# Idle matmuls and a new order of loads in the first stage of a one-core transformer block

## The chip, the core and the metric

The kernel runs on one core of one Trainium2 chip. The metric is the device time of one execution in microseconds (us); less is better. A core has five engines with instruction queues of their own: TensorE (PE in the profile, with its weight loads as PEld), VectorE (DVE), ScalarE (ACT), GpSimd (POOL) and SyncE (SP), which here only issues loads and stores to the DMA engines.

## What is computed

One block on x [256, 2048], all in float32, with a conditioning vector c [2048]:

```python
mod = jax.nn.silu(c) @ w_ada + b_ada              # 2048 -> 6 * 2048
shift_m, scale_m, gate_m, shift_f, scale_f, gate_f = split(mod, 6)
h = rms_norm(x, pre_norm_mix) * (1 + scale_m) + shift_m
q_n, k_c, ..., q_m, k_m, v_m = split(h @ w_in)    # eleven projections
o = concat(nsa_mixer(...), moba_mixer(...)) @ w_o
x = x + gate_m * rms_norm(o, post_norm_mix)
h = rms_norm(x, pre_norm_ffn) * (1 + scale_f) + shift_f
f = square(relu(h @ w_up)) @ w_down
x = x + gate_f * rms_norm(f, post_norm_ffn)
```

What matters for this change is the first line and the two after it, up to the first projections, and the last line.

## The kernel before, in words

**Order of the work.** The kernel is a list of units. A unit has a load (its DMA, issued on SP's queue into one of 5 raw buffers of 1 MB), a prep (work on what was loaded) and a main (its products). `Stream.run` (L108) issues loads in list order as raw buffers come free, preps up to four units ahead, and mains in order. The framework then lays out the order on each engine when the kernel is built: by priority, which follows the order of issue and is raised inside `tc.high_priority()`, among what its own plan holds to be ready. So a late-issued small instruction can stand early (L253 belongs to a later stage and runs at 1.37 us), but on the chip each engine takes its instructions in the order laid out.

**The modulation sums.** `shift` and `scale` for a group of k-tiles of h (M_MODS, L47: groups of 2, 4, 4, 4 and 2 tiles of 128 columns) are the product of silu(c) with a strip of w_ada. silu(c) is `csil` [128, 16], one column for each of the 16 k-tiles of the 2048 rows. `gemv_units` (L289) loads the strip (units of 4 or 2 k-tiles, SP at L305) and VectorE adds it up, `acc += w * csil[:, k]` (L318 for the first k-tile, L323 for the others). For the first group alone the k-tiles of M_DIRECT (L51) go to TensorE instead: `column_sums` (L352) runs 2 * nk = 4 matmuls of one column each into one PSUM bank, with w as the stationary side (L359); in the trace these are 8 instructions, since a float32 matmul stands there as two and a transpose as one. At the end of the group (`reduce`, L368) the running sum goes through the same function against a column of ones, another 8. The bank is opened by a matmul of the bias with the identity (L356). L389 and L390 then give `red`, and `main` (L393) modulates the transposed x with it (L400, L414). Later groups are reduced by transposes (L377) and split into a high and a low float32r part (L417, L418).

**x.** `x_units` (L566), one for each half t of 128 rows: load (L573), squares with their sum on ScalarE into `junk` (L579), 1/rms by `rstd_of` (L265: reduce, multiply-add, power on GpSimd), scaling on VectorE (L584), then 16 transposes through PSUM (L283; the identity they need is made by POOL at the start, masks.py:199) and copies by ScalarE (L285). `junk` and the running sum `acc` share one buffer (pool gp, tag "ga", one slot), so each waits for the one before it.

**The first products.** The projections of the first two k-tiles are done in plain float32 (M_PLAIN, L497): in_kv, in_kw, in_qn, in_vm, in_km, in_qm, with 1 MB of w_in each (0.5 for kw). The loads of the second modulation group (mods[1], eight loads of 1 MB and a last unit that reduces) are put between them by `spread` (L1000): in_kv, M0, M1, in_kw, M2, M3, in_qn, M4, M5, in_vm, M6, M7, in_km, in_qm in order of loads. Later products are `products` (L548): three float32r matmuls of high and low parts, whose weights are split by ScalarE (L544) and VectorE (L545).

**The end.** The last products end with `down_done` (L1222: square and sum on ScalarE, gating product on VectorE) for each 512 columns n of each half t, and `finish` (L1232): the four partial sums are added (L269), L273, power (L274), four scalings (L1238) and the stores.

**Lines that the change touches:** M_DIRECT (L51), the constants and silu(c) (L202 to L214), `columns` (L216), `column_sums`, `direct` and `reduce` (L352 to L391), `x_units` (L575 to L589), the list of units (L970 to L1000), `down_done` and `finish`.

## Time and profile before

| | us |
|---|---|
| median of 3 runs (1189.11 to 1192.91) | 1190.44 |
| the profiled execution | 1188.98 |
| its span, first to last instruction | 1187.2 |
| PE busy, share of the span | 1154.3 (97%) |
| DVE busy, share of the span | 901.4 (76%) |
| ACT busy, share of the span | 592.8 (50%) |
| HBM read | 308.99 MB |

Times in the rows are us from the first instruction, mean durations ns where so marked. A row `12.62 0.59 PE L356 MATMUL modm0t<-cola,ident ... x2 [3.62 <-DVE cola L223]` reads: at 12.62, for 0.59 us, two instructions of line 356 on TensorE wrote modm0t from cola and ident, after 3.62 us idle that ended with VectorE's line 223. Engines with a q behind them are issues to a queue. PE's ends are modelled, so the distance between starts is the firmer number.

### The profile page before, as it was taken

To read this page: it belongs to the slowest core of one execution; us is meant where nothing else is said; L and a number is where in the kernel's file an instruction comes from. 1 tells how busy PE (TensorE), PEld (TensorE's weight loads), DVE (VectorE), ACT (ScalarE), POOL (GpSimd) and SP (SyncE) were. 2 spreads that over 40 slices of the span, in tenths; PEclk is the share of its full clock that TensorE was granted. 3 is DMA by queue.
4 is the path that set the end of the run, shared out by engine and by line. 5 is a ranking of instruction groups with operands and counts; after the bars stand their busy time and mean duration, and the time that the engine had idled before them with its cause. 6 is when DMAs were issued, how large, how long until landed. Compare 5 with 4: busy or idle time off the path is not lost.

```text
span 1187.2 us, 14413 instructions
## 1 busy us (share of the span) xinstructions
PE 1154.3 (97%) x5411; PEld 935.7 (79%) x5411; DVE 901.4 (76%) x1111; ACT 592.8 (50%) x908; POOL 13.5 (1%) x23
## 2 busy tenths in 40 slices
PE   5999999999999998999999999999999999999997
PEld 4468888877777786888888888888888888888885
DVE  5679999889999988777888986666576666665573
ACT  4353444438746658565343344767444434444441
POOL 1000000000000001000000000000000000000000
PEclk9999999999999999999999999999999999999999
DMA  9999998775867985988878976545677777775541
GB/s 333 370 394 326 334 362 295 238 281 176 316 213 258 327 337 200 367 285 305 290 249 300 315 248 204 172 152 208 238 244 270 255 258 264 259 268 187 203 142 71
DMA packets 92601, 312.03 MB, mean 263 GB/s; under 512 B 6306, under 2 KB 14962, under 8 KB 79602
## 3 DMA queue, kind: packets, MB, share of 16 engines
q1 hardware_dynamic: 92324, 311.04, 74.7%
q8 instruction: 42, 0.69, 0.2%
q14 instruction: 27, 0.22, 0.1%
q10 hardware_dynamic: 208, 0.07, 0.0%
HBM read 308.99 MB, written 2.10 MB: 262 GB/s over the span
## 4 chain that ended last, share of the span: by engine, by line
PE 88%; DVE 7%; ACT 1%; issue 1%; DMA 1%; POOL 0%; SPq 0%; DVEq 0%; POOLq 0%; ACTq 0%
PE dps L550 10%; PE dps L551 10%; PE dps L549 10%; PE up L551 9%; PE up L550 9%; PE up L549 9%; PE wo L550 2%; PE wo L549 1%; PE wo L551 1%; PE ft L1146 1%; PE in_qm L551 1%; PE in_qm L549 1%; PE in_qm L550 1%; PE in_km L549 1%; PE in_km L550 1%
## 5 line engine op out<-in xcount | busy, mean ns | idle before, releaser
L323 DVE SCALAR_TENSOR_TENSOR modm<-modm,csil,modm 128x1024 f32<-128x1024 f32 (+1 forms) x72 | 78.3, 1087 | 9.4 <-DMA modm<-in_w_ada_dram 8.0
L323 DVE SCALAR_TENSOR_TENSOR modf<-modf,csil,modf 128x1024 f32<-128x1024 f32 x60 | 76.8, 1280 | 5.6 <-DMA modf<-in_w_ada_dram 5.2
L1162 DVE TENSOR_TENSOR facc<-up,facc 128x512 f32<-128x512 f32 x96 | 61.5, 685 | 19.2 <-PE up L551 19.2
L323 DVE SCALAR_TENSOR_TENSOR gatef<-gatef,csil,gatef 128x1024 f32<-128x1024 f32 x32 | 40.6, 1280 | 1.7 <-DMA gatef<-in_w_ada_dram 1.7
L323 DVE SCALAR_TENSOR_TENSOR gatem<-gatem,csil,gatem 128x1024 f32<-128x1024 f32 x32 | 40.3, 1275 | 0.0
L1202 DVE TENSOR_TENSOR flo<-facc,fhi 128x512 fp32r<-128x512 f32 x32 | 21.8, 686 | 2.0 <-ACT fhi L1201 2.0
L1201 ACT CAST fhi<-facc 128x512 fp32r<-128x512 f32 x32 | 19.7, 624 | 5.3 <-PE up L550 1.9
L1164 ACT ACTIVATE facc<-facc 128x512 f32<-128x512 f32 x32 | 18.4, 623 | 2.8 <-DVE facc L1162 2.8
L1160 ACT COPY facc<-up 128x512 f32<-128x512 f32 x32 | 18.0, 586 | 1.7 <-PE up L551 1.0
L545 DVE TENSOR_TENSOR up_13lo<-up,up_13hi 128x1024 fp32r<-128x1024 f32 x8 | 9.8, 1226 | 11.5 <-ACT up_13hi L544 11.5
L545 DVE TENSOR_TENSOR up_14lo<-up,up_14hi 128x1024 fp32r<-128x1024 f32 x8 | 9.8, 1226 | 11.1 <-ACT up_14hi L544 11.1
L1151 ACT ACTIVATE facc<-ft 128x512 f32<-128x512 f32 x32 | 17.1, 586 | 0.4 <-PE ft L1146 0.2
L1146 PE MATMUL ft<-ident,facc 128*128 128x128 f32 x128 | 16.8, 273 | 0.0
L1146 PEld LDWEIGHTS ft<-ident,facc 128*128 128x128 f32 x128 | 14.7, 140 | 2.6 <-ACT facc L1151 0.4
L544 ACT CAST up_7hi<-up 128x1024 fp32r<-128x1024 f32 x8 | 8.4, 1056 | 14.2 <-PE up L551 14.2
L544 ACT CAST up_11hi<-up 128x1024 fp32r<-128x1024 f32 x8 | 8.4, 1056 | 14.2 <-PE up L551 14.2
L544 ACT CAST up_10hi<-up 128x1024 fp32r<-128x1024 f32 x8 | 8.4, 1056 | 13.3 <-PE up L551 13.3
L544 ACT CAST up_6hi<-up 128x1024 fp32r<-128x1024 f32 x8 | 8.4, 1056 | 13.3 <-PE up L551 13.3
L544 ACT CAST up_14hi<-up 128x1024 fp32r<-128x1024 f32 x8 | 8.4, 1049 | 12.6 <-PE up L551 12.6
L544 ACT CAST up_9hi<-up 128x1024 fp32r<-128x1024 f32 x8 | 8.4, 1056 | 12.1 <-DVE up_8lo L545 6.7
L544 ACT CAST up_8hi<-up 128x1024 fp32r<-128x1024 f32 x8 | 8.4, 1054 | 11.7 <-PE up L551 11.7
L544 ACT CAST up_5hi<-up 128x1024 fp32r<-128x1024 f32 x8 | 8.4, 1056 | 11.2 <-PE up L551 7.8
(2266 smaller groups left out, 3966.4 us busy)
## 6 DMA issues: line engine op xcount, KB each, us to landing
up<-in_w_up_dram SPq DMA_DIRECT2D x64, 1024.0 KB, 5.2
dn<-in_w_down_dram SPq DMA_DIRECT2D x64, 1024.0 KB, 5.0
modf<-in_w_ada_dram SPq DMA_DIRECT2D x64, 512.0 KB, 6.2
modm<-in_w_ada_dram SPq DMA_DIRECT2D x48, 512.0 KB, 7.1
gatem<-in_w_ada_dram SPq DMA_DIRECT2D x16, 1024.0 KB, 5.5
wo<-in_w_o_dram SPq DMA_DIRECT2D x16, 1024.0 KB, 6.3
gatef<-in_w_ada_dram SPq DMA_DIRECT2D x16, 1024.0 KB, 4.9
modm<-in_w_ada_dram SPq DMA_DIRECT2D x32, 256.0 KB, 6.0
```

What stands on the lines that cost most here:

```text
L323: nc.vector.scalar_tensor_tensor(part, w[:, j:j + step], csil[:, k:k + 1], part, ALU.mult, ALU.add)
L544: nc.scalar.copy(hi[:, 0:n], src)
L545: nc.vector.tensor_sub(lo[:, 0:n], src, hi[:, 0:n].bitcast(F32))
L549: nc.tensor.matmul(o, shi, whi, start=first, stop=False)
L550: nc.tensor.matmul(o, shi, wlo, start=False, stop=False)
L551: nc.tensor.matmul(o, slo, whi, start=False, stop=last)
L1146: nc.tensor.transpose(b[:, (2 * i + t) * P:(2 * i + t + 1) * P], f[:, t, (2 * j + i) * P:(2 * j + i + 1) * P], ident)
L1160: nc.scalar.copy(dst, b)
L1162: nc.vector.tensor_add(dst, b, dst)
L1164: nc.scalar.activation(dst, dst, AF.Relu)
L1201: nc.scalar.copy(hi, f)
L1202: nc.vector.tensor_sub(lo, f, hi.bitcast(F32))
```

## The change

Seven edits:

- silu(c) gets a buffer of its own, `sig`, in the pool and tag of the squares' `junk`, so the squares wait for it; the loads of b_ada and the two norm vectors move from the top into `load_columns`, issued behind the first load of w_ada, and `columns` becomes a unit between the second and third loads of the first group.
- `keep_warm` issues transposes of data at hand into a PSUM bank that nobody reads: 56 of the identity at the start, 24 of x behind the second half's transposes, and 4 of the weights behind each direct k-tile.
- M_DIRECT names six k-tiles (2, 5, 8, 11, 13, 14) in place of three, so ten are left to VectorE.
- The bias of the first group is added by VectorE behind the sums and no longer by a matmul ahead of them.
- The second half of x is scaled by ScalarE.
- The second group's loads are put at fixed places: in_kv, M0, in_kw, M1, in_qn, M2, M3, in_vm, M4, in_km, M5, M6, in_qm, M7 in order of loads, the reducing unit behind in_qm's first k-tile.
- At the end, the sum of squares of the first three column blocks is reduced and scaled once n = 2 is done, and the last block takes one multiply-add and the power.

```diff
--- before.py
+++ after.py
@@ -48,7 +48,9 @@
 
 M_PLAIN = 2
 
-M_DIRECT = (3, 7, 11)
+M_DIRECT = (2, 5, 8, 11, 13, 14)
+
+WARM = (56, 24, 4)
 F_MODS = (4, 4, 4, 4)
 F_GROUPS = ((0, 4), (4, 8), (8, 12), (12, 16))
 
@@ -203,15 +205,26 @@
     stageb = accp.tile([64, P], F32, tag="acc", name="stageb")
     stagec = accp.tile([16, P], F32, tag="acc", name="stagec")
     nc.scalar.dma_start(stagec, c.rearrange("b (r p) -> (b r) p", p=P))
-    nc.scalar.dma_start(stagea[0:96, :], b_ada.rearrange("b (r p) -> (b r) p", p=P))
-    nc.scalar.dma_start(stagea[96:112, :], g_pm.rearrange("b (r p) -> (b r) p", p=P))
-    nc.scalar.dma_start(stagea[112:128, :], g_pf.rearrange("b (r p) -> (b r) p", p=P))
     with tc.high_priority():
         pc = bank("pconst0")
         nc.tensor.transpose(pc[:, 0:16], stagec, ident[0:16, 0:16])
-        sigmoid_parts(csil, pc[:, 0:KD])
-        nc.vector.reciprocal(csil, csil)
-        nc.vector.tensor_mul(csil, csil, pc[:, 0:KD])
+
+        sig = gp.tile([P, KD], F32, tag="ga", name="csig")
+        sigmoid_parts(sig, pc[:, 0:KD])
+        nc.vector.reciprocal(sig, sig)
+        nc.vector.tensor_mul(csil, sig, pc[:, 0:KD])
+    warm = mbank("warm")
+
+    def keep_warm(src, n):
+        for i in range(n):
+            nc.tensor.transpose(warm[:, (i % 4) * P:(i % 4 + 1) * P], src, ident)
+
+    keep_warm(ident, WARM[0])
+
+    def load_columns():
+        nc.scalar.dma_start(stagea[0:96, :], b_ada.rearrange("b (r p) -> (b r) p", p=P))
+        nc.scalar.dma_start(stagea[96:112, :], g_pm.rearrange("b (r p) -> (b r) p", p=P))
+        nc.scalar.dma_start(stagea[112:128, :], g_pf.rearrange("b (r p) -> (b r) p", p=P))
 
     def columns():
 
@@ -351,16 +364,16 @@
 
         def column_sums(w, v, stop):
 
-            if "b" not in sums:
+            fresh = "b" not in sums
+            if fresh:
                 sums["b"] = bank(f"{name}t")
-                nc.tensor.matmul(sums["b"][:, 0:2 * nk].rearrange("p (s k) -> p s k", s=2), ident,
-                                 bias[:, :, ks], start=True, stop=False, skip_group_check=True)
             for i in range(2 * nk):
                 nc.tensor.matmul(sums["b"][:, i:i + 1], w[:, i * P:(i + 1) * P], v,
-                                 start=False, stop=stop, skip_group_check=True)
+                                 start=fresh and i == 0, stop=stop, skip_group_check=True)
 
         def direct(k, w):
             column_sums(w, csil[:, k:k + 1], False)
+            keep_warm(w[:, 0:P], WARM[2])
 
         units = gemv_units(name, base + k0 * P, W, True, min(1024 // W, 4), acc, first,
                            direct if tag == "m" and k0 == 0 else None)
@@ -385,9 +398,10 @@
                 return lambda k: (red[:, k - k0:k - k0 + 1], red[:, nk + k - k0:nk + k - k0 + 1])
             with tc.high_priority():
                 column_sums(acc.t, one, True)
-                b = sums["b"]
-                nc.vector.tensor_mul(red[:, nk:], b[:, nk:2 * nk], gcol[:, ks])
-                nc.vector.tensor_copy(red[:, 0:nk], b[:, 0:nk])
+                nc.vector.tensor_add(red.rearrange("p (s k) -> p s k", s=2),
+                                     sums["b"][:, 0:2 * nk].rearrange("p (s k) -> p s k", s=2),
+                                     bias[:, :, ks])
+                nc.vector.tensor_mul(red[:, nk:], red[:, nk:], gcol[:, ks])
             return lambda k: (red[:, k - k0:k - k0 + 1], red[:, nk + k - k0:nk + k - k0 + 1])
 
         def main():
@@ -581,12 +595,17 @@
             with tc.high_priority():
                 r = rstd_of(f"xr{t}", ss)
                 for v in st["x"]:
-                    nc.vector.tensor_scalar(v, v, r, None, ALU.mult)
+                    if t:
+                        nc.scalar.mul(v, v, r)
+                    else:
+                        nc.vector.tensor_scalar(v, v, r, None, ALU.mult)
 
         def main():
             if t == 0:
                 xnm.extend(pair(f"xnm{i}") for i in range(KD // 2))
             transposed(f"xt{t}", lambda k: st["x"][k // 8][:, (k % 8) * P:(k % 8 + 1) * P], xnm, t)
+            if t:
+                keep_warm(st["x"][1][:, 0:P], WARM[1])
 
         u = Unit(None, prep, main)
         u.begin = load
@@ -967,7 +986,6 @@
     k0s = np.cumsum((0,) + M_MODS).tolist()
     mods = [mod_units("m", k0, n, xnm, hstat) for k0, n in zip(k0s, M_MODS)]
     xu = [x_units(0), x_units(1)]
-    columns()
     gm = gate_units("m", g_qm, gate_m)
 
     def call(f):
@@ -991,13 +1009,16 @@
 
     def load_first():
         load0()
+        load_columns()
         for u in xu:
             u.begin()
 
     m0[0].load = load_first
-    stream.add(xu + m0)
+    stream.add(xu + m0[:2] + [Unit(None, columns)] + m0[2:])
     base = flat(in_units(n, 0, 2) for n in ("kv", "kw", "qn", "vm", "km")) + turn0[:2]
-    stream.add(spread(base, mods[1], 1, len(base) - 1))
+    for j, at in enumerate((2, 5, 8, 9, 12, 15, 16, 18, 19)):
+        base[at:at] = mods[1][j]
+    stream.add(base)
     base = turn0[2:] + flat(in_units(n, 2, 6) for n in ("km", "vm", "qn", "kw")) + turn1[:4]
     base.insert(3, Unit(None, late_constants))
     stream.add(spread(base, mods[2], 0, len(base) - 3))
@@ -1227,12 +1248,26 @@
             nc.vector.tensor_add(b, dps[0, 0], b)
         junk = pair("junk").rearrange("p a b -> p (a b)")
         nc.scalar.activation(junk, b, AF.Square, accum_out=fsq[t][:, n:n + 1])
+        if n >= 2:
+            with tc.high_priority():
+                final_rstd(n, t)
         nc.vector.tensor_mul(fg[n][:, t, :], b, gate_f["G"][:, n * 512:(n + 1) * 512])
+
+    frstd = [[sm.tile([P, 1], F32, name=f"fr{t}{i}", bufs=1) for i in range(2)] for t in range(NT)]
+
+    def final_rstd(n, t):
+
+        s, r = frstd[t]
+        if n == 2:
+            nc.vector.tensor_reduce(s, fsq[t][:, 0:3], axis=AX.X, op=ALU.add)
+            nc.vector.tensor_scalar(s, s, 1.0 / D, EPS, ALU.mult, ALU.add)
+        else:
+            nc.vector.tensor_scalar(r, fsq[t][:, 3:4], 1.0 / D, s, ALU.mult, ALU.add)
+            nc.gpsimd.tensor_tensor(r, r, mhalf, ALU.pow)
 
     def finish(t):
         x2 = x2h["x"]
-        with tc.high_priority():
-            r = rstd_of(f"fr{t}", fsq[t])
+        r = frstd[t][1]
         for n in range(4):
             cs = slice(n * 512, (n + 1) * 512)
             nc.vector.scalar_tensor_tensor(x2[:, t, cs], fg[n][:, t, :], r, x2[:, t, cs],
```

## Rows read from the trace of the kernel before

**Rows 1.** The page, parts 1 and 4: busy time and the chain that ended last.
```profile
PE 1154.3 (97%) x5411; PEld 935.7 (79%) x5411; DVE 901.4 (76%) x1111; ACT 592.8 (50%) x908; POOL 13.5 (1%) x23
...
PE 88%; DVE 7%; ACT 1%; issue 1%; DMA 1%; POOL 0%; SPq 0%; DVEq 0%; POOLq 0%; ACTq 0%
```

**Rows 2.** Timeline of PE, 0 to 48 us: start, us, instruction, count, [idle before].
```profile
12.62 0.59 PE L356 MATMUL modm0t<-cola,ident 128*128 128x4 f32 x2 [3.62 <-DVE cola L223]
...
16.38 5.01 PE L283 MATMUL xt<-ident,x 128*128 128x128 f32 x21
...
24.99 1.84 PE L359 MATMUL modm0t<-one,modm 128*128 128x1 f32 x8
27.84 9.44 PE L497 MATMUL in_kv<-in_kv,xnm 128*128 128x512 f32 x16 [1.01 <-ACT xnm L414]
37.12 3.78 PE L497 MATMUL in_kw<-in_kw,xnm 128*128 128x268 f32 x16
```

**Rows 3.** Timeline of PE, 38 to 130 us.
```profile
49.12 7.11 PE L497 MATMUL in_vm<-in_vm,xnm 128*128 128x512 f32 x16 [1.36 <-DMA in_vm<-in_w_in_dram]
56.06 1.04 PE L377 MATMUL modm2t<-ident,modm 128*128 128x128 f32 x8
...
70.51 0.79 PE L549 MATMUL in_qm<-in_qm_2hi,modm2hi 128*128 128x512 f32 x1
```

**Rows 4.** Timeline of PEld, the weight loads, 0 to 48 us.
```profile
32.27 0.31 PEld L497 LDWEIGHTS in_kv<-in_kv,xnm 128*128 128x128 f32 x1 [0.52 <-issue]
32.83 0.19 PEld L497 LDWEIGHTS in_kv<-in_kv,xnm 128*128 128x128 f32 x1 [0.24 <-issue]
```

**Rows 5.** Windows: length, busy PE, PEld, DVE, ACT, POOL, clock, DMA share, GB/s.
```profile
12.00:92.00 80.00, 77.01 (x261) 50.08 (x262) 57.26 (x65) 33.93 (x63) 3.88 (x6) 1.00 1.04 380
92.00:126.00 34.00, 33.28 (x171) 27.40 (x169) 33.80 (x42) 15.54 (x21) 0.00 (x0) 1.00 0.92 320
126.00:230.00 104.00, 104.00 (x511) 88.04 (x512) 95.53 (x123) 43.67 (x51) 1.81 (x1) 1.00 0.91 309
```

**Rows 6.** Timeline of all engines, 0 to 40 us.
```profile
1.04 0.29 POOL masks.py:199 TENSOR_SCALAR_AFFINE_SELECT ident<-ident 128x128 f32<-128x128 f32 x1
...
10.91 0.75 DVE L584 TENSOR_SCALAR x<-x,xr 128x1024 f32<-128x1024 f32 x1 [0.41 <-POOL xr L274]
...
11.22 1.06 ACT L579 ACTIVATE xj<-x 128x1024 f32<-128x1024 f32 x1
...
15.92 8.91 DVE L323 SCALAR_TENSOR_TENSOR modm<-modm,csil,modm 128x512 f32<-128x512 f32 x11
```

**Rows 7.** Timeline of ACT, 55 to 96 us.
```profile
64.97 1.04 ACT L544 CAST in_qm_2hi<-in_qm 128x1024 fp32r<-128x1024 f32 x1
...
88.50 1.06 ACT L544 CAST in_vm_2hi<-in_vm 128x1024 fp32r<-128x1024 f32 x1 [1.80 <-DMA in_vm<-in_w_in_dram]
```

**Rows 8.** Timeline of DVE, 55 to 96 us.
```profile
54.50 1.28 DVE L323 SCALAR_TENSOR_TENSOR modm<-modm,csil,modm 128x1024 f32<-128x1024 f32 x1
...
60.60 0.69 DVE L418 TENSOR_TENSOR modm2lo<-xnm,modm2hi 128x512 fp32r<-128x512 f32 x1 [2.22 <-ACT modm2hi L417]
...
66.05 1.23 DVE L545 TENSOR_TENSOR in_qm_2lo<-in_qm,in_qm_2hi 128x1024 fp32r<-128x1024 f32 x1 [1.62 <-ACT in_qm_2hi L544]
...
86.73 1.22 DVE L545 TENSOR_TENSOR in_km_5lo<-in_km,in_km_5hi 128x1024 fp32r<-128x1024 f32 x1 [0.81 <-ACT in_km_5hi L544]
...
91.66 1.37 DVE L633 TENSOR_TENSOR km<-in_km,km 128x512 f32<-128x512 f32 x2 [2.51 <-PE in_km L551]
```

**Rows 9.** Timeline of all engines, from 1160 us.
```profile
1179.20 0.16 DVE L269 TENSOR_REDUCE fr<-fsq 128x1 f32<-128x4 f32 x1 [2.03 <-ACT junk L1229]
1179.28 0.68 DVE L1230 TENSOR_TENSOR fg<-dps,gatef 128x512 f32<-128x512 f32 x1
...
1180.19 0.55 POOL L274 TENSOR_TENSOR fr<-fr,mhalf 128x1 f32<-128x1 f32 x1 [9.83 <-DVE fr L273]
1180.77 2.74 DVE L1238 SCALAR_TENSOR_TENSOR x<-fg,fr,x 128x512 f32<-128x512 f32 x4 [0.75 <-POOL fr L274]
```

## The prediction, before the run

> **What bounds the kernel now.** I read the page first, for the bound of the whole: TensorE is busy 97% of the span and is 88% of the chain that ended last [rows 1]. So time is won only where TensorE waits, does the wrong work or runs slowly. The change touches two such places, the first 30 us and the last 10.
>
> The timeline of TensorE shows the first place [rows 2]. Until 12.6 us it does almost nothing. From there to 26.8 it works without a real gap, but at helpers: 32 transposes of x, 24 one-column instructions for the direct k-tiles, 8 for the running sum. The first product starts at 27.84. These helpers are slow. 21 transposes take 5.01 us and 8 sums 1.84, so 0.21 to 0.24 us each; eight transposes at 56 us take 1.04, or 0.13 with the last one's tail in it [rows 2, 3]. The weight loads show where that ends [rows 4]: the loads of the first products stand 0.85 us apart up to 32.27 and 0.43 from 32.83 on. So up to 32.3 us TensorE runs at the lower of its two levels (1.2 GHz), and afterwards at the higher (2.4). The clock column of the windows reads 1.00 there too [rows 5]; it doesn't show this early stretch, so I go by the spacing. What it did before the rise: 14 us of transposes and one-column sums, then 4.8 us of 512-column products.
>
> The windows show the second limit [rows 5]. From 12 to 92 us the DMA share is 1.04: the loads follow each other without a gap, whatever the engines do. From 92 to 126 DMA falls to 0.92 and VectorE is busy 33.8 of 34.0 us. From 126 to 230 TensorE is busy 104 of 104. So an earlier start has to pass a stretch bound by loads and one bound by VectorE before it reaches the TensorE-bound rest, where it is kept.
>
> **The change, part by part.** *silu(c) ahead of x, six direct k-tiles, x of the second half on ScalarE.* The exponential stood behind two squares of x on ScalarE; the buffer that sig shares with the junk of these squares now puts it first. That frees direct sums earlier, but VectorE's running sum needs the same buffer after the last square, which ends at 12.28 [rows 6], so it starts no earlier than now. Its list shrinks: 13 k-tiles become 10, at 8.91/11 = 0.81 each, 2.4 us; the scaling of the second half of x leaves it too, two of about 0.75, 1.5 us [rows 6]. It ended at 24.83; it could end at 20.9, or later if the loads are later, so between 20.9 and 24.8. ScalarE takes two passes of 1024 at 1.06, 2.1 us, ahead of the second half's copies; its last square sets when they can start, and it had gaps behind the transposes. I cost them at nothing on the path; without that cover they are 2.1 us on the second half's transposes. The columns' loads stay on the same queue and are 64 KB.
>
> *Idle matmuls.* TensorE's queue between x and the last sums grows: 32 transposes, 6 x (8 sums + 4 idle) = 72, 24 idle, then 8 sums, 136 instructions. The 56 ahead of it run in time that was empty. At the high level, half of the low spacing or 0.11 each, the queue takes 15.0 us; at the low one, 0.22, 29.9. Before, 64 of them took 14.2 (12.62 to 26.83). So everything hangs on whether the 56 raise the clock. They are back to back from when the identity is made, 1.33 us [rows 6], 12 us long at the low spacing; no row of this trace has such a row of transposes, and the denser part of the 14 us above was shorter and interrupted. I take it that they do: each streams 128 columns through all 128 rows, as a quarter of a product's instruction does, without gaps. That is my weakest step, and the slow rival below is its failure. Then x, whose first half is scaled by 10.91 + 0.75 = 11.7 as now [rows 6], is followed by 15.0 us: sums end at 26.7, and with the 1.0 us from there to the first product (26.83 to 27.84 now) it starts at 27.7. If VectorE decided alone, it would be 20.9 + 0.9 + 1.0 = 22.8. I take 27.5, near the first, because TensorE's queue is the longer. So the earlier start is almost nothing; what is won is the clock: 16 products took 9.44 and take 16 x 0.43 = 6.9, so kw starts at 34.4 where it was 37.12 [rows 2]. From there to the end of the first group is 70.51 - 37.12 = 33.4 us, with a wait of 1.36 for in_vm's load in it [rows 3]; 32.0 without. TensorE could begin the second group at 66.4.
>
> *Weights ahead of the second group's loads.* Each product load comes up to two loads earlier and the last two of the group's sums later. That removes the in_vm wait, counted above. But the loads in front of the second group's first weights (in_qm, k = 2) are the same set in another order, and DMA is full, so these still arrive at 64.97 [rows 7]; six loads lie between in_vm's arrival at 49.1 and that, 2.65 us each. The split ends at 66.05 + 1.23 = 67.28 [rows 8]. The last sums of that group now arrive two loads before, at 59.7. From the last sum's start to the end of the first split state took 54.50 to 60.60 + 0.69, 6.8 us [rows 8]: 66.5. So the second group starts at 67.3 against 70.51 [rows 3], **3.2 us earlier**, loads deciding, not 4.1. A first product as late as 28.4 would do as well.
>
> Does it pass VectorE's stretch? VectorE stands idle 0.81 us before 86.73 and 2.51 before 91.66, the first behind a cast, the second until TensorE ends in_km [rows 8]. The next work, in_vm's weights, is there at 88.50 [rows 7]. So 3.3 us of idle can go, if the planner's order uses it; 2.5 if only the second gap goes. I keep 3.2, since the cast of the first gap stands in ScalarE's queue among the copies of TensorE's results, and 2.5 as the low end.
>
> *The sum of squares at the end.* The chain is reduce 1179.20, multiply-add, power 1180.19, last scaling 1180.77 [rows 9]. The reduce and the 0.68 us gating product that ran between it and the multiply-add drop out: the multiply-add goes to 1179.20, as long as the reduce or 0.16, the power to 1179.5, the scaling, 0.58 behind it as now, to 1180.1. **0.7 us**, bounds 0.3 (planner puts the product first) and 0.8. The two small steps for n = 2 run under products.
>
> *Bias added behind the sums:* two instructions leave the front of TensorE's queue (12.62, 0.59 [rows 2]), and one small VectorE step changes its kind in the 1.0 us tail; nothing, within 0.3 either way.
>
> Sum: 3.2 + 0.7 = 3.9 us. The profiled execution took 1188.98 us, with a span of 1187.2; the median of the runs is 1.46 above it. 1190.44 - 3.9 = 1186.5.
>
> **The rivals.** *Given back (0.24).* The planner lays out another order, or VectorE's stretch is fixed by its work: 33.8 of 34.0 us leave no room. For it: VectorE's low slack there. Against: its two gaps before 92 us, which I trace to TensorE. Then the end's 0.7 and some 0.5 are left: 1189.2.
>
> *The idle transposes don't raise the clock (0.16), slower.* Place: TensorE's queue from 1.3 to 27 us. The 56 take 56 x 0.22 = 12.3, to 13.6; then 29.9; sums end at 43.5, the first product is at 44.5, 16.7 late. Since TensorE then leads nothing, only the in_vm wait (1.4) and the end (0.7) come back: 1190.44 + 14.6 = 1205.0. For it: 14 us of transposes and sums at the low spacing. Against: interrupted, and half of them one column wide. It decides when more than some 8 us of the queue run low, each costing half: the second group then starts no earlier than before. The Trainium skill ("TensorE: Matmul & The Clock Gate", Part 4: PE-mode transpose) states that a transpose doesn't count as busy for the clock as a matmul does; by that rule it would be these 1205.0. This trace's rows don't contradict it, and no row settles it.
>
> *Loads don't hold it (0.10).* If the products' loads overtake enough, and the direct sums finish by 24, the first product is at 25 and the second group begins near 64: 6 us and the end's 0.7, 1183.7. Against: the full DMA share.
>
> **How the numbers follow.** Forecast 0.50, its own range 1185 to 1188. The range of all: from 1182.5 (loads don't hold) to 1192 (given back; single runs of before reached 1192.91); the slow case, 0.16, and a tail stay out. 0.3% is 3.6 us, about what this kernel's runs can tell from no change. Faster by more: three quarters of the forecast and the third rival, 0.48. Within: the rest of the forecast and given back, 0.36. Slower: 0.16.
>
> **What would show it.** Right: idle transposes 0.11 apart before 10 us; in_kv's 16 products in 6.9 us; the second group's first split product near 67, right behind its weights' split; no wait at in_vm; VectorE busy through from 89; power at 1179.5 less the shift. Wrong: transposes of x 0.21 apart; a first product after 31; VectorE idle for nothing at 92 to 126 while TensorE waits for a split; a gain at 70 us that is gone at 126.

## The result, and the profile after

The changed kernel takes 1198.64 us (median of 8 executions, 1196.94 to 1205.56) where the kernel before takes 1190.43 beside it (8 executions, 1189.11 to 1194.17): ratio 1.0074, 95% interval 1.0048 to 1.0101. It is **slower by some 8 us**; 1186.5 was forecast, with a range up to 1192.0.

The profiled execution of after took 1196.94 us (span 1195.2), that of before 1188.98 (span 1187.2). I follow the difference of 8.0 us between these two along TensorE.

First its timeline up to the first product (start, length, instruction, count, idle before):

```profile
3.42 7.99 PE L220 MATMUL warm<-ident 128*128 128x128 f32 x56
12.35 1.02 PE L371 MATMUL modm0t<-csil,modm 128*128 128x1 f32 x8 [0.94 <-DMA modm<-in_w_ada_dram]
13.23 0.63 PE L220 MATMUL warm<-ident,modm 128*128 128x128 f32 x4
14.51 1.05 PE L371 MATMUL modm0t<-csil,modm 128*128 128x1 f32 x8 [0.65 <-DMA modm<-in_w_ada_dram]
15.43 0.64 PE L220 MATMUL warm<-ident,modm 128*128 128x128 f32 x4
15.90 0.27 PE L232 MATMUL pconst<-ident,stagea 128*128 128x128 f32 x1
16.01 1.20 PE L296 MATMUL xt<-ident,x 128*128 128x128 f32 x8
...
22.87 2.46 PE L220 MATMUL warm<-ident,x 128*128 128x128 f32 x21
...
27.26 1.03 PE L371 MATMUL modm0t<-one,modm 128*128 128x1 f32 x8
28.15 0.63 PE L220 MATMUL warm<-ident,modm 128*128 128x128 f32 x4
29.98 8.83 PE L511 MATMUL in_kv<-in_kv,xnm 128*128 128x512 f32 x16 [1.20 <-ACT xnm L428]
```

The helpers run at twice the pace of before: the last 8 sums take 1.03 us here and 1.84 in [rows 2]. So the 56 did raise the clock. Yet x's transposes start at 16.01 (13.07 before), though x's first half is scaled by 11.42: the direct sums of k-tiles 2 and 5 stand ahead of them in the queue, wait for their loads, and hold up TensorE. The first product comes at 29.98, **2.1 us later** than in [rows 2]. Part of that lies behind the last sum, on VectorE:

```profile
28.33 0.16 DVE L401 TENSOR_TENSOR modm0red<-modm0t,cola 128x4 f32<-128x4 f32 x1 [4.68 <-PE modm0t L371]
28.41 0.75 DVE L331 TENSOR_SCALAR modm<-modm,csil 128x1024 f32<-128x1024 f32 x1
29.08 0.15 DVE L404 TENSOR_TENSOR modm0red<-modm0red,cola 128x2 f32<-128x2 f32 x1
```

The bias is now added (L401) before the multiplication (L404) can run, and the planner laid a step of the next group's sum between the two. From the end of the last sum to the first product are 1.7 us (28.29 to 29.98), where before had 1.0.

The windows of after (length, busy PE, PEld, DVE, ACT, POOL, clock, DMA share, GB/s) show that the clock, once high, doesn't stay so:

```profile
12.00:28.00 16.00, 15.00 (x132) 14.27 (x132) 7.52 (x15) 7.04 (x18) 3.05 (x6) 1.00 1.07 369
28.00:33.00 5.00, 3.80 (x12) 1.87 (x12) 4.49 (x7) 0.60 (x1) 0.00 (x0) 0.78 0.98 352
...
40.00:70.00 30.00, 30.00 (x82) 14.70 (x81) 13.40 (x13) 8.55 (x16) 0.00 (x0) 1.00 0.99 355
70.00:80.00 10.00, 5.10 (x15) 3.35 (x14) 8.28 (x11) 7.39 (x11) 0.00 (x0) 0.83 0.83 303
```

It falls as the products begin (0.78), so in_kv takes 8.83 us and not the 6.9 I counted on. With in_vm's wait of 1.36 us [rows 3] gone, the last plain product ends at 70.77 (71.07 before): 0.3 us ahead. What follows is the loss. The timelines of the three engines, 60 to 80 us:

```profile
63.49 1.28 DVE L336 SCALAR_TENSOR_TENSOR modm<-modm,csil,modm 128x1024 f32<-128x1024 f32 x1 [0.45 <-DMA modm<-in_w_ada_dram]
68.65 1.29 DVE L392 TENSOR_REDUCE modm2red<-modm2t 128x4 f32<-128x512 f32 x2 [3.87 <-PE modm2t L390]
69.85 0.74 DVE L331 TENSOR_SCALAR modm<-modm,csil 128x1024 f32<-128x1024 f32 x1
...
70.63 1.28 DVE L336 SCALAR_TENSOR_TENSOR modm<-modm,csil,modm 128x1024 f32<-128x1024 f32 x1
71.83 0.16 DVE L397 TENSOR_TENSOR modm2red<-modm2red,cola 128x4 f32<-128x4 f32 x1
...
74.21 0.69 DVE L432 TENSOR_TENSOR modm2lo<-xnm,modm2hi 128x512 fp32r<-128x512 f32 x1 [0.97 <-ACT modm2hi L431]
...
72.09 1.58 ACT L428 ACTIVATE xnm<-xnm,modm2red 128x256 f32<-128x256 f32 x3 [8.44 <-DVE modm2red L397]
...
74.59 1.03 ACT L558 CAST in_qm_2hi<-in_qm 128x1024 fp32r<-128x1024 f32 x1
...
62.86 5.31 PE L511 MATMUL in_qm<-in_qm,xnm 128*128 128x512 f32 x12
68.01 1.04 PE L390 MATMUL modm2t<-ident,modm 128*128 128x128 f32 x8
68.88 1.88 PE L511 MATMUL in_qm<-in_qm,xnm 128*128 128x512 f32 x4
75.67 1.65 PE L563 MATMUL in_qm<-in_qm_2hi,modm2hi 128*128 128x512 f32 x3 [4.90 <-ACT in_qm_2hi L558]
...
78.39 0.47 PE L565 MATMUL in_qm<-in_qm_2hi,modm2lo 128*128 128x512 f32 x1
78.70 0.40 PE L564 MATMUL in_qm<-in_qm_2lo,modm2hi 128*128 128x512 f32 x1
```

VectorE's sum for the second group is complete at 64.77 (63.49 + 1.28). Its transposes on TensorE (modm2t) come at 68.01, because they stand in the queue behind 12 of in_qm's 16 plain products. From there the chain goes through VectorE, where two steps of the next group's sum (2.0 us) run between its own, through ScalarE, where in_qm's cast waits behind the modulation, to 75.67. Only four products cover it: **TensorE stands for 4.90 us**, and the next products run at the low clock (window 70 to 80: 0.83). The group starts 5.2 us later than in [rows 3].

The account between the two profiles is the distance between the same products, as it stands at each place: -0.3 us at the last plain product; +6.2 at the end of the second group's first k-tile (4.9 of the wait, 1.6 of the low clock behind it), and still +6.2 at 373 us, so that VectorE's stretch from 92 to 126 us neither gave nor took; +7.0 at 384 us and +8.65 at 427, behind two more dips of the clock that the profile of before doesn't have. The shorter end takes 0.65 off: +8.0. The end, as forecast:

```profile
1187.84 0.21 DVE L1265 TENSOR_SCALAR fr<-fsq,fr 128x1 f32<-128x1 f32 x1 [1.91 <-ACT junk L1250]
...
1188.13 0.55 POOL L1266 TENSOR_TENSOR fr<-fr,mhalf 128x1 f32<-128x1 f32 x1 [9.09 <-DVE fr L1265]
1188.72 2.74 DVE L1273 SCALAR_TENSOR_TENSOR x<-fg,fr,x 128x512 f32<-128x512 f32 x4
```

From the start of the multiply-add to the last scaling are 0.88 us; from the reduce to it were 1.57 in [rows 9], 0.69 more.

### The profile page after: what moved, and what is told of

Same layout as the page of the kernel before. It is cut to its first block, busy times and chain, and to the rows that moved or that the text cites. A ratio compares the mean times of both kernels' runs of the same rounds, so it can differ in the third digit from the quotient of the medians.

```text
span 1195.2 us, 14664 instructions
## 1 busy us (share of the span) xinstructions
PE 1166.3 (98%) x5537; PEld 947.9 (79%) x5537; DVE 897.1 (75%) x1108; ACT 595.1 (50%) x910; POOL 12.6 (1%) x23
## 4 chain that ended last, share of the span: by engine, by line
PE 87%; DVE 7%; issue 2%; ACT 2%; DMA 1%; POOL 0%; ACTq 0%; DVEq 0%; POOLq 0%
PE up L563 9%; PE up L564 9%; PE up L565 9%; PE dps L563 9%; PE dps L564 9%; PE dps L565 9%; PE wo L564 2%; PE wo L565 2%; PE wo L563 1%; PE ft L1167 1%; PE in_qm L563 1%; PE in_qm L565 1%; PE in_qm L564 1%; PE in_km L564 1%; PE in_kv L564 1%
## 5 line engine op out<-in xcount | busy, mean ns | idle before, releaser
L336 DVE SCALAR_TENSOR_TENSOR modm<-modm,csil,modm 128x1024 f32<-128x1024 f32 (+1 forms) x69 | 75.7, 1097 | 19.1 <-DMA modm<-in_w_ada_dram 18.2
L1183 DVE TENSOR_TENSOR facc<-up,facc 128x512 f32<-128x512 f32 x96 | 61.5, 683 | 18.8 <-PE up L565 18.7
```

The lines of the kernel that those rows point to most:

```text
L336: nc.vector.scalar_tensor_tensor(part, w[:, j:j + step], csil[:, k:k + 1], part, ALU.mult, ALU.add)
L1183: nc.vector.tensor_add(dst, b, dst)
```

## The experiments

Eighteen kernels. "First" is the start of the first product and "split" that of the second group's first split product, in the one profiled execution of each, in us; "clock" is the granted clock from 12 to 28 us there. Times are medians of 4 to 12 executions; the kernel before, run beside them, had 1189.2 to 1190.4.

| kernel | time | ratio to before (95%) | first | clock | split |
|---|---|---|---|---|---|
| before | 1190.43 | | 27.84 | | 70.51 |
| after | 1198.64 | 1.0074 (1.0048 to 1.0101) | 29.98 | 1.00 | 75.67 |
| e1 after, old order | 1195.38 | 1.0053 (1.0033 to 1.0073) | 36.41 | 0.59 | 79.85 |
| e2 before, new order | 1193.95 | 1.0041 (1.0028 to 1.0054) | 27.13 | | 72.67 |
| e3 after, no idle matmul | 1203.80 | 1.0121 (1.0105 to 1.0137) | 33.24 | | 79.81 |
| e4 before, the 56 | 1196.06 | 1.0057 (1.0045 to 1.0069) | 34.11 | 0.59 | 75.70 |
| e5 as e1, the 56 alone | 1196.46 | 1.0049 (1.0031 to 1.0068) | 32.15 | 0.60 | 76.11 |
| e6 before, third order | 1192.25 | 1.0019 (1.0005 to 1.0033) | 27.10 | | 68.26 |
| e7 before, new end | 1189.38 | 0.9999 (0.9984 to 1.0014) | 27.20 | | 69.97 |
| e8 after, third order | 1198.16 | 1.0064 (1.0041 to 1.0088) | 30.00 | 1.00 | 70.22 |
| e9 after, four chunks | 1205.18 | 1.0118 (1.0087 to 1.0149) | 37.29 | 0.62 | 84.11 |
| e10 after, 70 for 56 | 1199.32 | 1.0084 (1.0066 to 1.0102) | 30.97 | 1.00 | 76.43 |
| e11 before, third order, chunks, end | 1192.84 | 1.0023 (1.0011 to 1.0034) | 27.34 | | 69.64 |
| e12 as e8, chunks, 70 | 1197.01 | 1.0054 (1.0037 to 1.0071) | 37.61 | 0.64 | 79.20 |
| e13 after, late direct | 1203.54 | 1.0112 (1.0098 to 1.0127) | 36.16 | 0.79 | 81.77 |
| e14 as e8, late direct | 1201.66 | 1.0091 (1.0073 to 1.0109) | 38.54 | 0.66 | 79.93 |
| e15 as e14, the 56 alone | 1196.45 | 1.0063 (1.0044 to 1.0082) | 33.25 | 0.69 | 75.18 |
| e16 as e14, no idle | 1202.16 | 1.0100 (1.0087 to 1.0113) | 36.04 | | 76.73 |
| e17 start mended, old order | 1195.66 | 1.0051 (1.0035 to 1.0068) | 32.97 | 0.71 | 75.67 |
| e18 after, x on VectorE | 1202.56 | 1.0098 (1.0077 to 1.0120) | 35.94 | 0.57 | 82.30 |

(Where no clock stands, the records of the clock begin behind the window or, in e2 and e6, inside it, at 20.0 and 18.8 us; before its first record the view reads 1.00, which says nothing.)

### The order of loads: e1, e2, e6, e8

e1 and e2 exchange one line between the kernels:

```diff
-    stream.add(spread(base, mods[1], 1, len(base) - 1))
+    for j, at in enumerate((2, 5, 8, 9, 12, 15, 16, 18, 19)):
+        base[at:at] = mods[1][j]
+    stream.add(base)
```

> The changed kernel with the load order of the second group of sums put back as before. Theory A (order): the new order puts the reducing unit behind nearly all of the group's products, so its chain (last sum at 64.77, split state 10 us later) stands open before the second group. With the old order the first split product comes back from 75.67 to 70.5 to 72, and the time to 1190 to 1193. Theory B (idle work): the 24 and the 4s lengthen TensorE's queue and hold raw buffers, whatever the order; then the first split product stays past 74 and the time stays at 1196 or more.

> The kernel before with only the new load order. Theory A: in_vm's wait of 1.4 us goes, but the reduction's chain stands open: the first split product at 74 to 76 in place of 70.51, slower by 4 to 6 us, 1194 to 1197. Theory B: the order itself costs nothing; first split product at 69 to 70.5, 1188.5 to 1190.5.

The new order alone makes the kernel before 0.4% slower, close to what theory A gave, with the split product at 72.67 somewhat ahead of it. The old order takes about a quarter off the median of the changed kernel's loss (1.0053 for 1.0074), but the intervals overlap, and its split product came at 79.85, later and not earlier (why, below). So e1 decides neither way between its theories. In e2's timeline of PE the same wait stands:

```profile
65.01 1.04 PE L377 MATMUL modm2t<-ident,modm 128*128 128x128 f32 x8
65.89 1.88 PE L497 MATMUL in_qm<-in_qm,xnm 128*128 128x512 f32 x4
72.67 1.65 PE L549 MATMUL in_qm<-in_qm_2hi,modm2hi 128*128 128x512 f32 x3 [4.91 <-ACT in_qm_2hi L544]
```

All seven kernels with the new order have this wait at 4.90 or 4.91 us, wherever their starts lie, and none of the others has it. So it comes neither from the loads nor from the clock but from the laid-out order, in which four products of 0.47 us follow the transposes. The third order puts the reducing unit ahead of in_qm:

```diff
-    for j, at in enumerate((2, 5, 8, 9, 12, 15, 16, 18, 19)):
+    for j, at in enumerate((2, 5, 6, 9, 12, 13, 15, 16, 18)):
```

> The kernel of before with a third order: weights ahead of the second group's loads as in the change, but the last three of the group's eight loads one place earlier and the reducing unit ahead of in_qm's plain products, not behind them. Theory A (what costs 5 us in the changed order is the reducing chain, laid behind TensorE's last 16 plain products): the split state is ready before in_qm's weights (k = 2), the second group's first split product comes at 67 to 69 us against 70.51 before and 74.46 in the new order, and the time is 1186 to 1188.5. Rival (VectorE's stretch from 92 to 126 us takes back whatever the second group gains): 1188.5 to 1190, with the first split product at 67 to 69 all the same. Rival (any order with the weights first holds back the sums, so the chain is late here too): first split product after 71, 1190 to 1194.

> The changed kernel with the third order (reducing unit ahead of in_qm's plain products) and all else as changed. Theory A alone: the wait of 4.9 us ahead of the second group goes, 1192 to 1195 beside 1198.6 of the changed kernel; what is left above before comes from the first product at about 30 us and the returns of the low clock. By the theory that the idle matmuls and the direct k-tiles hold back the sums so far that the order makes no difference: 1196 to 1199.

e6, timeline of PE:

```profile
60.92 1.04 PE L377 MATMUL modm2t<-ident,modm 128*128 128x128 f32 x8
61.79 7.03 PE L497 MATMUL in_qm<-in_qm,xnm 128*128 128x512 f32 x16
68.26 1.49 PE L549 MATMUL in_qm<-in_qm_2hi,modm2hi 128*128 128x512 f32 x4
...
84.43 0.80 PE L549 MATMUL in_km<-in_km_4hi,modm2hi 128*128 128x512 f32 x1 [3.15 <-ACT in_km_4hi L544]
```

The wait is gone and the group starts 2.25 us earlier than before, as theory A has it (the new order had 72.67, not the 74.46 that the expectation names); but the time, 1192.25, is longer than any of the three theories gave. At 84.43 TensorE waits 3.15 us for in_km's weights (k = 4), cast at 83.33 as they land. In the kernel before the same cast and its product are these:

```profile
82.06 1.05 ACT L544 CAST in_km_4hi<-in_km 128x1024 fp32r<-128x1024 f32 x1 [4.55 <-PE in_qm L551]
```

```profile
83.17 0.49 PE L549 MATMUL in_km<-in_km_4hi,modm2hi 128*128 128x512 f32 x1
```

The row puts the cast's wait down to a product that ends in the same instant; the load, issued at 72.1, took 9.9 us and landed at 82.0, and in e7, which has the loads of before, the row of this cast names the load. So before had been at its loads there already: a second group that starts earlier only waits for them. All seven kernels with the third order wait at this product, 1.77 to 3.15 us.

e8 has no 4.90 us either, and its split product came at 70.22. But its median is 1198.16, within what the second theory gave and not to be told from the 1198.64 of the changed kernel. Its five executions lie from 1190.31 to 1200.84, and the longer they took, the lower was their mean granted clock (0.997, 0.992, 0.989, 0.988, 0.986). The profiled one is the fastest; there the clock stayed high from 34 us to the last products, and 1.3 us are left of the loss. In e1 the fastest of nine took 1190.16, also at the highest clock (0.996). This suggests that either order, with the clock kept, brings the changed kernel near the kernel before; it doesn't show it.

### The buffers: e9, e11, e12

Why do the weights land later in the new orders? e6's windows (here GB/s is the last number) and its waits of the queue that issues loads (us, times, longest):

```profile
36.00:40.00 4.00, 4.00 (x18) 3.02 (x17) 0.61 (x1) 1.94 (x4) 0.00 (x0) 1.00 0.52 138
```

```profile
SPq L305 <- PE in_kv L497: 7.6, 1, 7.6
```

The DMA engines stand half idle: five buffers are held by plain weights that came early and wait for their products, and the next load waits 7.6 us for in_kv's. In the changed kernel the share is 0.82 from 36 to 44 us. I gave in_qn's and in_kw's plain weights four free accumulator chunks (the main lines of the edit):

```diff
-                st["raw"] = rawtile(f"{name}_{ks[i0]}")
+                if own(i0):
+                    st["own"] = [chunk(f"{name}_{k + kk}").rearrange("p a b -> p (a b)") for kk in range(2)]
...
```

> The changed kernel with its own order, but the plain weights of in_qn and in_kw go into four free accumulator chunks and not into two of the five load buffers. Theory A2 (with the weights ahead, five buffers are held by weights that wait for their products, so that the DMA engines stand idle and the second group's weights come late: in_qm, k = 2, landed at 68.64 us against 64.95 before): in_qm, k = 2, lands at 65 to 66.5, the loads move 365 GB/s or more from 30 to 60 us (339 in the changed kernel), the last sums of the second group come at 60 to 61.5 and its first split product at 71.5 to 73.5 against 75.67; the time is 2 to 4 us below the changed kernel's 1198.6. Rival (the loads are late because DMA is full, not for want of buffers): in_qm, k = 2, lands at 68 or later and the time stays at 1197 to 1200.

> The kernel of before with the third order (weights first, the reducing unit ahead of in_qm's plain products), the four chunks for in_qn's and in_kw's plain weights, and the new end; no idle matmuls and no other part of the change. Theory A2: the first split product at 67 to 68.5 us with no wait for in_km's weights behind it (3.15 us in the third order without the chunks), and what is won there, 2 to 3 us, kept through 126 us; with the end's 0.7, 1186 to 1188 where before has 1189.5. Rival (VectorE's stretch from 92 to 126 us, or the low clock, takes it back): 1188.5 to 1191.

> The changed kernel with three things mended: the third order, the four chunks for in_qn's and in_kw's plain weights, and 70 idle transposes. If the theories on the chain, the buffers and the pause in front of x hold and nothing else costs time: 1186 to 1189, with the first split product of the second group at 67 to 69 us. If the idle matmuls behind x and the direct sums still hold back the first product (29.98 against 27.84) and that isn't made good: 1189 to 1192. Rival (the low clock returns by chance at later places): 1192 to 1198.

All three missed what was hoped of them; e12's time lies where its last rival had it. e9's first product came at 37.29 with the clock lost, and decides nothing about buffers. e11 starts the split products at 69.64, but waits again for in_km (2.19 us, 85.53): the hole in the loads had moved, to 52 to 60 us (share 0.71), behind in_vm's buffer. That the buffers are what delays the loads is shown by these waits; that more of them would pay is not.

### The idle matmuls: e3, e4, e5, e10

e3, e5 (this one with the old order too) and e10 change one line of after; e4 adds three to before:

```diff
-WARM = (56, 24, 4)
+WARM = (0, 0, 0)
...
+WARM = (56, 0, 0)
...
+WARM = (70, 24, 4)
...
+    warm = mbank("warm")
+    for i in range(56):
+        nc.tensor.transpose(warm[:, (i % 4) * P:(i % 4 + 1) * P], ident, ident)
```

> The changed kernel with no idle transposes at all (0, 0, 0). TensorE's 88 helper instructions then run at the lower clock, 0.21 each. Theory A: first product at 30 to 33, in_kv's products slow for some 4 us, and the first split product near 75 to 79, the time 1196 to 1200. Theory B (the idle work is what costs): first product at 27 or earlier, no 24 and no 4s in the queue and in_qn's load issued before 27; first split product near 70, the time 1190 to 1192.

> The kernel before with only the 56 transposes of the identity at the start. The clock rises near 7 us, as in the changed kernel, and x's transposes stand 0.11 apart. Theory A (loads decide up to the second group): the first product moves from 27.84 to about 26.5 to 27.5, but in_vm's load still lands near 49, its wait grows from 1.4 to 3 to 5 us, the first split product stays within 0.5 of 70.5, and the time within 1 us of before. Rival: the clock's gain is kept, first split product at 67 to 68, 1187 to 1188.

> The changed kernel with the loads and the reducing unit in their old order, and of the idle matmuls only the 56 ahead of x (none behind x, none behind the direct k-tiles). Its neighbour is the kernel with the old order and all idle matmuls, 1195.38. By the theory that the 48 idle matmuls in the queue cost time (about 2.46 us for 24 and 0.65 to 0.8 for each four, at the profile's spacing, ahead of the last sums): first product some 4 us earlier than there, 1190 to 1193. By the theory that the clock decides and the 48 hold it up: as late as there or later, 1195 to 1199, with the profile's clock at the low level for most of 15 to 33 us.

> The changed kernel with 70 idle transposes of the identity in place of 56, so that they reach up to the first work on x and the direct sums (the 56 end at 11.0 to 11.8 us, the next work is at 12.4). Theory C (the high clock is lost in some executions in the pause behind the 56, and those are the slow ones: three of eight runs at 1201 to 1205.6): all runs at 1196 to 1199, none above 1200, median 1197, and the clock in the profile high from 6 or 8 us to about 30. Rival (it is lost in the later stretches of one-column sums, or by chance): runs above 1200 in the same share, median 1198 to 1200. By either, up to 0.6 us is added to the first product.

Without any, the changed kernel is 5 us slower still (e3), so they do help it. The kernel before with the 56 is 7 us slower (e4), but that isn't their price alone: the planner now put VectorE's copy of the columns behind steps of its sum, and TensorE waited 8.41 us for it (20.43). Both theories for e4 missed. What limits the gain stands in the clock column: in all thirteen profiles with such transposes the clock was high by 9 us, but in only three (after, e8, e10) still so, without a break, at 28. In e1, whose queue up to the first product is that of after, it fell at the second group of sums; window and two rows of PE's timeline:

```profile
12.00:28.00 16.00, 14.69 (x75) 14.47 (x76) 7.62 (x15) 5.70 (x15) 3.05 (x6) 0.59 1.07 370
```

```profile
12.68 1.02 PE L371 MATMUL modm0t<-csil,modm 128*128 128x1 f32 x8 [0.79 <-DMA modm<-in_w_ada_dram]
...
14.84 1.87 PE L371 MATMUL modm0t<-csil,modm 128*128 128x1 f32 x8 [0.64 <-DMA modm<-in_w_ada_dram]
```

The same instructions, and the first product 6.4 us later: whether the level survives the thin stretch behind the 56 varies from execution to execution. That fits the spread of after (five executions up to 1200, three from 1201 to 1205.6, two of these at a mean clock of 0.985 where the fastest has 0.993). With the old order from first product to first split product are 42.7 us in before and 43.4 in e1, so a late start isn't made good.

e5, without the 48 behind the 56, has its first product at 32.15, 4.3 us ahead of e1 as the first theory gave, with the clock low from 15 us as the second gave. Its median is no lower than e1's (1.0049 and 1.0053), so the 48 show no effect on the time here.

e10 closes the pause between the 56 and x. Its profile kept the clock, but its four executions reach 1202.4, as the rival gave, and e12, with the same 70, lost it: that pause alone isn't the cause.

### The queue in front of x: e13 to e18

e13 has this edit alone; e14 to e16 have the third order too, with all idle matmuls, the 56 and none:

```diff
-M_DIRECT = (2, 5, 8, 11, 13, 14)
+M_DIRECT = (8, 9, 11, 12, 13, 14)
```

> The changed kernel with the six direct k-tiles moved from 2, 5, 8, 11, 13, 14 to 8, 9, 11, 12, 13, 14 and nothing else, so that x's first 16 transposes stand ahead of all direct sums in TensorE's queue. Theory D (the sums of k-tiles 2 and 5, waiting for their loads, hold back x and thin the queue until the clock falls back): x's first transpose at 11.7 to 12.5 us against 16.01, first product at 25.5 to 27.5 against 29.98, the clock high from 6 to 9 us up to that product, and no run above 1200; the chain ahead of the second group is not mended, so 1193 to 1196 beside 1198.6. Rival (the 48 idle matmuls make the queue long, or the clock falls back by chance): first product at 29 or later, 1197 to 1200, with runs near 1205.

> The changed kernel with the late direct k-tiles and the third order (reducing unit ahead of in_qm's plain products). If theory D and theory A hold and add up: first product at 25.5 to 27.5, first split product of the second group at 66 to 68.5, 1186 to 1189. If in_km's weights (k = 4) then land at 84 as in the third order elsewhere, so that TensorE waits there and the start is taken back: 1188.5 to 1191. Rival (the clock by chance): 1192 to 1198.

> As the late direct k-tiles with the third order, but of the idle matmuls only the 56 ahead of x. If the 48 behind them only lengthen the queue: first product as early or up to 2 us earlier than with them (25.3, where in_kv's weights land), and 0 to 2 us less. If they are what holds the clock up between 13 and 27 us: the clock is low again before the first product in the profile, and the time is 1 to 4 us more.

> As the late direct k-tiles with the third order, without any idle matmul: what the rest of the change does by itself. By the queue worked out at the low clock: 32 transposes and 56 sums at 0.22 are 19.4 us from 12.0 on, first product at 32 to 33, in_kv at the low clock, so 3 to 5 us later than with the 56: 1191 to 1196. If loads and VectorE set the second group's start whatever the first products do: within 1.5 us of the kernel with the 56.

e13, timeline of PE:

```profile
12.21 1.04 PE L296 MATMUL xt<-ident,x 128*128 128x128 f32 x8
14.62 0.66 PE L296 MATMUL xt<-ident,x 128*128 128x128 f32 x4 [1.37 <-DVE cola L233]
17.11 0.66 PE L220 MATMUL warm<-ident,modm 128*128 128x128 f32 x4 [1.83 <-DMA modm<-in_w_ada_dram]
17.60 0.60 PE L296 MATMUL xt<-ident,x 128*128 128x128 f32 x4
18.04 2.56 PE L371 MATMUL modm0t<-csil,modm 128*128 128x1 f32 x16
...
36.16 6.17 PE L511 MATMUL in_kv<-in_kv,xnm 128*128 128x512 f32 x10 [0.73 <-ACT xnm L428]
```

x's transposes do start at 12.21, but the first product gets later, not earlier, and the time is longer than both theories gave: now they wait for a bank that VectorE frees late (the columns' copy), then behind idle transposes that wait for a load, and the clock falls at 19 us. ScalarE's copies stand behind its two scalings of x (14.03 to 16.22 us); in e15 x's fourth group of transposes waits 1.52 us for them. So theory D fell: with the direct sums out of the way, x meets the next obstacles. e15 and e16 differ by 5.7 us, what the 56 are worth at most with this queue (in e16 ScalarE's first square also waits 5.95 us for silu(c), which the planner then lays out later). In e14 the other 48 seem to take it back (1201.66 against 1196.45), since at the low clock they lengthen the queue; but the intervals of the two overlap, and e5 and e1 show no such difference. The times of all three missed their ranges.

```diff
-                    if t:
-                        nc.scalar.mul(v, v, r)
-                    else:
-                        nc.vector.tensor_scalar(v, v, r, None, ALU.mult)
+                    nc.vector.tensor_scalar(v, v, r, None, ALU.mult)
```

This is e18; e17 has it too, with the old order, the columns at their old place with a bank of the other kind, `M_DIRECT = (12, 13, 14, 15)`, the 56 alone, and these and x's transposes at high priority.

> The changed kernel with the old order of loads and the old place of the columns, their result in another kind of bank, both halves of x scaled on VectorE, x's transposes put first by priority, direct sums for k-tiles 12 to 15 alone, and of the idle matmuls the 56 (of which 20 now stand between x's halves). The new end stays. If the queues in each other's way were what made the first product late: x's first transpose at 11 to 12 us, first product at 25.3 (in_kv's weights) to 27.5, and 1186.5 to 1189 beside about 1189.5 of before. If TensorE's thin work between 13 and 19 us lets the clock fall back: first product at 27 to 29, 1189 to 1193.

> The changed kernel with x's second half scaled on VectorE as before, and nothing else undone. If ScalarE's two passes of 1.06 us ahead of the copies cost time: first product 0.5 to 2 us earlier than 29.98, 1196 to 1198. If they lie beside other work (the direct sums ahead of x's transposes decide): first product at 29.5 to 30.5, or at 35 where the clock falls back, and 1197 to 1200.

Neither gains. In e18's profile the clock fell at 13.4 us, before x's second half is scaled, so it says nothing about ScalarE's two passes. In e17 x starts at 12.78, but TensorE, with no idle matmul left to put there, waits 2.85 us for the k = 12 load and has lost the clock:

```profile
14.87 2.35 PE L220 MATMUL warm<-ident 128*128 128x128 f32 x20
20.08 0.55 PE L372 MATMUL modm0t<-csil,modm 128*128 128x1 f32 x2 [2.85 <-DMA modm<-in_w_ada_dram]
...
32.97 9.19 PE L512 MATMUL in_kv<-in_kv,xnm 128*128 128x512 f32 x16 [1.14 <-ACT xnm L429]
```

### The end: e7

`final_rstd` is added to the kernel before, and nothing else:

```diff
+        if n >= 2:
+            with tc.high_priority():
+                final_rstd(n, t)
...
-            r = rstd_of(f"fr{t}", fsq[t])
+        r = frstd[t][1]
```

> The kernel of before with the sum of squares at the end alone: sums of three of the four parts taken early, one multiply-add and the power behind the last part. By the chain at the end: from the end of the last product to the end of the span 8.75 us before, 8.05 here, and 0.7 us less, 1188.3 to 1188.9 beside 1189.2. By the rival that the chain at the end isn't bound there: no difference beyond 0.2 us in that stretch.

The time is 0.5 us lower and can't be told from no change (ratio 0.9999). In the profile the step is there: from the end of the last product to the end of the span are 8.10 us (8.75 before; 7.9 to 8.1 in all profiles with the new end, 8.7 to 8.8 in all without). No version was faster than the kernel before by what can be measured.

## Why the prediction was wrong, by its steps

**The idle transposes raise the clock**, called my weakest step: right. They stand 0.14 us apart over all 56, between the 0.21 of the low level and the 0.11 of the high, and 0.11 behind them. By the Trainium skill ("TensorE: Matmul & The Clock Gate", Part 4: PE-mode transpose) a transpose doesn't count as busy for the clock as a matmul does; here float32 transposes raised it in all thirteen profiles, and the measurement decides.

**"What is won is the clock": failed.** I let the level, once raised, last. It fell in every profile before in_kv was through; in ten of thirteen already by 20 us, with helpers at the low spacing behind it. My slow rival's 1205.0 lies near e3 without the 56 (1203.8) and near two executions of after (1205.3, 1205.6), but that is chance: its sum has the first product at 44.5, and e3 has it at 33.24 and loses the rest later.

**The queue: 136 instructions from 11.7 on, 15.0 us.** Its length was right, its start wrong. From x's first transpose to the end of the last sums are 12.3 us for the 112 instructions in between, 0.11 each. But 24 of the 136 and the columns' transpose stand ahead of x and wait for loads, so x starts at 16.0. I had taken the direct sums as behind x because the list has them there, and hadn't asked when k-tiles 2 and 5 land. The tail behind the sums was sized at 1.0 us, with the bias at "nothing, within 0.3 either way": it took 1.7 in after. In the kernels without the four idle transposes behind the last direct k-tile it took 1.15 (e3, e5), so some 0.15 are the bias's own and the rest is the step laid in between. The first product was forecast at 27.5 and measured 29.98.

**"DMA is full, so these still arrive at 64.97": failed.** in_qm's weights (k = 2) landed at 68.64, though in after that isn't what TensorE waited for: their cast stood in ScalarE's queue until 74.59. The mean share of 1.04 in [rows 5] hid that loads are issued only as buffers come free; weights taken early hold them longer. And I tested the earlier start against in_vm's weights (88.50 in [rows 7]), not against in_km's (k = 4), whose cast in before runs from 82.06 to 83.11 with its first product at 83.17: no slack at all. e6, e8 and e11 lose what they had won there.

**From the last sum to the first split state, "6.8 us", ending at "66.5": the costliest failure between the two profiles.** The last sum started at 63.49, not at 59.7, since its load came later too. The chain was sized from before, where it stood ahead of in_km's products and had them as cover. Behind in_qm's products it took from 63.49 to the split at 74.9, 11.4 us, and 4.90 of it uncovered, with the low clock behind them. I had named the moved step, but not what stands in front of it on TensorE and VectorE, nor how few products were left behind it. Of the steps that failed this one cost most: a term sized 6.8 us, to end ahead of the weights, measured 11.4 and ended 6.3 us behind their landing (68.64). e2 (put in: +0.4%) and e6 (order mended: the wait gone, but 0.2% slower than before still) show it in the kernel before; in the changed kernel (e8) the wait goes as well, but the median doesn't fall.

**Right:** in_vm's wait went, and the end gave 0.7 us. ScalarE's two passes, costed at nothing, are hidden in after (13.69 to 15.88 us, x's next copies wait for TensorE until 16.65); e15 shows a price of 1.52 us once the cover goes.

**Not settled:** why the clock dips at about 375 and 424 us in some executions, which is 2.4 of the 8.0 us between the two profiles. after, e1, e2 and e6 have one or both dips, before, e7 and e8 none, with the same work there; e7 and e6 as kernels reach 1193.7 and 1195.7 in single executions. Nor was it found what exactly in the thin stretch from 12 to 20 us decides whether the level holds. No kernel has the third order with the direct k-tiles of the change and no idle matmul, so what the idle matmuls are worth once the order is mended was not measured.

## What to carry to other kernels

Before a reducing step is moved later so that loads may come earlier, count the products that will be left behind it to cover its chain, on every queue it passes; and ask what holds the buffers that the earlier loads take. A high clock bought with idle work has to be kept by the work that follows: if that stands waiting, the level may be gone before the products begin, and the idle work then only lengthens the queue. A mean DMA share near 1 says nothing about a single load: look at when it lands and who starts in the same instant.

## What was not expected of the hardware

Float32 transposes alone raise TensorE's clock: in all thirteen profiles it was high by 6.2 to 8.9 us, with one small transpose of c and the 56 (or 70) of the identity as the only work ahead. The level is easily lost: in ten of the thirteen it fell by 20 us, in stretches in which TensorE waits for a load, a bank or VectorE between transposes and one-column sums. The same instruction stream keeps it in one execution (after, 8 sums in 1.05 us at 14.51) and loses it in another (e1, 1.87 us at 14.84). It also rises unasked: in e2 and e6, without any idle work, it was high for part of x's own transposes (e2: 8 sums take 1.71 us at 13.80, 0.95 at 20.11 and 1.87 at 24.25), in before, e7 and e11, with the same instructions up to there, it was not. Behind the wait of 4.9 us in the middle of dense products it was low in all seven profiles that have it: in after the products run 0.43 us apart up to 78.4 us, where the split products of before stand 0.23 apart. Behind the shorter waits for in_km (1.77 to 2.40 us) it fell in four profiles (e11, e12, e14, e16) and held in two (e8, e15).
